# A two-layer decoder on one core: one shared block result kept in SBUF and added by VectorE, the turning block emptied by ScalarE, one chunk's bank taken from the other PSUM pool

## The chip, the core and the metric

The kernel runs on one core of a Trainium2 chip. The metric is the device time of one execution in microseconds. A core has TensorE (PE in the profile, with its weight loads as PEld), VectorE (DVE), ScalarE (ACT), GpSimd (POOL) and SyncE (SP). They run their own instruction streams and wait for each other on semaphores; data moves between DRAM and SBUF by DMA, and the matmuls write into PSUM, which here is eight banks of 128 x 512 fp32.

## The reference

Two layers of a hybrid decoder over 512 tokens of width 1024, all in fp32, and a final RMSNorm:

```
h   = RMSNorm(x)
z   = h @ W_in      # attn q,k,v | ret q,k,v,g | gate_a | gate_b
A   = sliding-window attention with rotary q/k and sinks
B   = retention with group norm and swish gate
y   = sigmoid(gate_a) * (A @ W_a) + sigmoid(gate_b) * (B @ W_b)
x   = x + y @ W_out
x   = x + relu(RMSNorm(x) @ W_up)^2 @ W_down     # 1024 -> 4096 -> 1024
```

The change touches the second half, the MLP (`W_up`, `W_down`), the first products of a layer (`W_in`, the attention's q) and the final RMSNorm.

## The kernel before

**Products.** fp32 operands are split into a high and a low part (`split_until`: ScalarE makes `hi` at L308, VectorE `lo` at L309; for activations L361/L362 and L364/L365), and each product is three matmuls, high x high, high x low and low x high (`products`, L354 to L356). Raw weights come by SP's queue into a ring of five tiles, `hi` and `lo` have rings of four; sums of weight blocks that are needed come from DRAM and are added with L267 and L290. The scheduler of the framework decides the order in which each engine takes its instructions, from the program's order and its own estimates.

**Banks.** Five of the eight PSUM banks belong to the pool `ps_mm`, three to `ps_aux`. `temp()` gives a 128 x 512 tile from a ring of seven in SBUF: who takes the eighth waits until the first one's readers are done, DMAs out of it among them.

**The start of a layer.** `group` takes four `ps_mm` banks for the products of k, v and two chunks of q (`put_k`, `put_v`, `put_q(0)`, `put_q(1)`), then `chunk` takes one bank each for q(2) and q(3). `rotate` reads a bank (L566, L567 by ScalarE, L570 by VectorE) and applies the rotary tables; `beside` spreads the results by SP's DMAs (L597). The scores are L705.

**The MLP.** It is cut into eight blocks e of hidden units. Each block has two `pair` products (up, with relu and square) and one `down` product. Both are multiplications of 2 x 2 blocks in seven products instead of eight, so the results share partial sums:

- `pair` holds three half banks a, e, b in `ps_mm`. It copies a to b on ScalarE (L1152), copies e to the tile `eu` (L1154), copies b there (L1157), and goes on accumulating in all three; L1159, L1164, L1166, L1167 and L1172 finish the squares.
- `down` holds four `ps_mm` banks a[0..1], c[0..1] and two `ps_aux` banks b[0..1]; b begins as a copy of a (L1234). It yields results (i, j, m), where i is the half of the tokens' columns, j and m choose one of four output blocks. Two of them are early: `early(1, 1)` from c and `early(0, 1)` from b are partial sums shared with later results; then come `put(0, 0)` from a, `put(0, 1)` from c, `put(1, 1)` from b and `put(1, 0)` from b, with another product into b before each of the last two.

**Adding** (blocks 0 to 6 of each layer): each of the twelve results of a block (six names, two values of m) is taken out of PSUM by ScalarE into a tile (L1276) and sent by POOL with an accumulating DMA into a DRAM tensor y (L1278). (1, 1) and (0, 1) are thus each sent twice, once for the early part and once for the late one. POOL waits before an accumulating DMA until the earlier one into the same place has landed.

**Ending** (block 7 of each layer): y comes back from DRAM (L1292) and VectorE adds the last results from PSUM (`add`, L1307). In layer 0 the early (1, 1) is still added by an accumulating DMA (L1303), `turn` transposes the results on TensorE (L1334) and adds them to x (L1340), and `carry`, which runs inside layer 1's first group, turns the half i = 1; behind it x is split into xh (L364) and xl (L365) for the next products. In layer 1 the Ending also makes the final RMSNorm: squares on ScalarE (L1315), the gain on VectorE (L1316), the root and its inverse, the scaling on VectorE for i = 1 (L1323) and on ScalarE for i = 0 (L1326), and the DMAs to the output.

Of the kernel before, what the change touches and what calls it, by code (L numbers as in the profile page):

```python
# [12 lines left out]
AF = mybir.ActivationFunctionType  # L13
ALU = mybir.AluOpType
# [4 lines left out]
T = 512  # L19
# [95 lines left out]
def decoder(ctx, tc, xT, x_first, w_in, w_a, w_b, w_out, w_up, w_pair, w_down, w_end, tables, decay, band, g_last, out):  # L115
    nc = tc.nc
# [19 lines left out]
    def bank(pool, name):  # L136
        return pool.tile([P, T], F32, tag=pool.name, name=name)
# [229 lines left out]
    xs = [(xh[:, k, :], xl[:, k, :]) for k in range(KD)]  # L367
# [4 lines left out]
    def advance(rate=1.0):  # L372

        credit[0] += rate
        while credit[0] >= 1.0:
            credit[0] -= 1.0
            while background:
                try:
                    next(background[0])
                    break  # L380
                except StopIteration:
                    background.pop(0)
# [2 lines left out]
        while background:  # L385
            advance()

    def chunk(name, layer, moving, evacuate, rate=1.0):

        hi, lo = unit(name, layer)  # L390
        n = len(moving)
        ps = bank(ps_mm, "mm")
        pairs = [((hi[:, k * P : (k + 1) * P], lo[:, k * P : (k + 1) * P]), moving[k]) for k in range(n)]
        advance(rate)
        products(ps, pairs[: n // 2], True, False)
        advance(rate)
        products(ps, pairs[n // 2 :], False, True)
        evacuate(ps)
# [150 lines left out]
    def layer_body(layer):  # L549
# [81 lines left out]
        def put_q(c):  # L631
            def put(ps):
                r = rotate(ps, attn_tabs, layer == 0 and c < 2)
                if c % 2 == 0:
                    qlo[:] = [big("qlo")]
                lo = qlo[0][:, c % 2, :]
                for g in range(N_KV):
                    nc.scalar.activation(q_s[g][:, c, :], r, AF.Copy)
                nc.vector.tensor_tensor(lo, r, f32(q_s[0][:, c, :]), ALU.subtract)
                for g in range(N_KV):  # L640
                    beside(g, q_s[g][:, c, :], lo)

            return put
# [6 lines left out]
            {0: squares, 1: rms_mix.prepare, 2: stats} if layer == 0 else {0: carried.pop(), 2: rms_mix.prepare, 3: stats},  # L650
        )
        chunk("w_in", layer, xs, put_q(2))
        chunk("w_in", layer, xs, put_q(3))
        turn_v()

        a_t = [slots.four() for _ in range(2)]
# [187 lines left out]
        class Head:  # L844


            def __init__(self, h):
                self.h = h
# [193 lines left out]
        last = layer == DEPTH - 1  # L1042
        y = dram.tile([P, NB, D], F32, name=f"y{layer}")
# [7 lines left out]
        factor, negative = (columns[:, i * NB : (i + 1) * NB] for i in range(2))  # L1051
        if last:
# [3 lines left out]
            last_gain = gain_tile[:, 0:2, :]  # L1056
# [199 lines left out]
        class Adding:  # L1256


            def __init__(self, e):
                self.e = e  # L1260

            def last_but_one(self):
                pass
# [2 lines left out]
                pass  # L1266

            def early(self, i, j, m, ps, sign):
                self.send(i, j, m, temp("eu"), ps, sign, last or self.e > 0)

            def put(self, i, j, m, ps, sign):
                self.send(i, j, m, temp("y"), ps, sign, last or self.e > 0 or j == 1)

            def send(self, i, j, m, t, ps, sign, add):
                block = 2 * j + m
                nc.scalar.activation(t, ps, AF.Copy, scale=(factor if sign > 0 else negative)[:, block : block + 1])  # L1276
                how = {"accum_op": ALU.add} if add else {}
                nc.gpsimd.dma_start(y[:, block, i * T : (i + 1) * T], t, **how)  # L1278

        class Ending:  # L1280


            def __init__(self):
                self.y, self.done = {}, set()
# [23 lines left out]

            def put(self, i, j, m, ps, sign):
                block = 2 * j + m  # L1310
                self.add(i, j, m, ps, (factor if sign > 0 else negative)[:, block : block + 1])
                if last:
                    v = self.y[i, j, m]
                    first, total, both = (sq[:, n * NB + block : n * NB + block + 1] for n in range(3))
                    nc.scalar.activation(temp("junk"), v, AF.Square, accum_out=both if i else first)  # L1315
                    nc.vector.tensor_tensor(v, v, last_gain[:, i, :], ALU.mult)  # L1316
# [6 lines left out]
                    nc.vector.tensor_scalar(v, v, total, None, ALU.mult)  # L1323
# [28 lines left out]
                    carried.append(self.carry)  # L1352

            def carry(self):
                for half in range(2):
                    for j in (1, 0):
                        self.turn(1, j, half, ps_aux)
                    for k in (4 + 2 * half, 5 + 2 * half):
                        scaled_input(k, g_mix + 2)
                for k in range(KD):  # L1360
                    squared_input(k, g_mix + 2)
                    nc.sync.dma_start(spill[:, k, :], x[:, k, :])
                late_box[0] = late_tile(F32R)
                slots.add(late_box[0])
# [200 lines left out]
```

## Time and profile before

| | |
|---|---|
| Runs | 1497.24, 1502.52, 1502.98 us; median 1502.52 |
| Profiled execution | 1501.42 us |
| Its span | 1499.7 us |
| Mean granted TensorE clock | 0.997 |
| DMA moved | 286.25 MB, mean 191 GB/s |

The span runs from the first to the last instruction; the profiled execution's own time has 1.72 us around it. In rows of a timeline the first number is the start in us from the span's start, the second the duration, and a bracket at the end names the idle time of the engine ahead of the instruction and what ended it. In a group's row stand its count, its busy time in us, the mean of one in ns, and the engine's idle time ahead of it. Matmul rows overlap: their pitch, not their duration, is what a product costs.

### The profile page before, as it was taken

To read this page: it belongs to the slowest core of one execution; us is meant where nothing else is said; L and a number is where in the kernel's file an instruction comes from. 1 tells how busy PE (TensorE), PEld (TensorE's weight loads), DVE (VectorE), ACT (ScalarE), POOL (GpSimd) and SP (SyncE) were. 2 spreads that over 40 slices of the span, in tenths; PEclk is the share of its full clock that TensorE was granted. 3 is DMA by queue.
4 is the path that set the end of the run, shared out by engine and by line. 5 is a ranking of instruction groups with operands and counts; after the bars stand their busy time and mean duration, and the time that the engine had idled before them with its cause. 6 is when DMAs were issued, how large, how long until landed. Compare 5 with 4: busy or idle time off the path is not lost.

```text
span 1499.7 us, 21303 instructions
## 1 busy us (share of the span) xinstructions
PE 1471.8 (98%) x7787; PEld 1265.7 (84%) x7787; DVE 1044.3 (70%) x1589; ACT 940.9 (63%) x1551; POOL 239.7 (16%) x334
## 2 busy tenths in 40 slices
PE   9999999999999999999999999999999999999997
PEld 7888888888889999998778888888888789888885
DVE  6878568654677777776977775677447677777665
ACT  7657355532568888887755563555325778877775
POOL 0101121101002222223001011111000212222230
PEclk9999999999999999999999999999999999999999
DMA  7654997668227888888836579876443488888883
GB/s 257 189 169 113 303 256 185 185 179 223 92 72 220 211 215 218 223 213 230 290 100 182 147 207 273 223 205 155 140 121 110 122 205 213 210 219 211 218 205 126
DMA packets 100472, 286.25 MB, mean 191 GB/s; under 512 B 11664, under 2 KB 11792, under 8 KB 96528
## 3 DMA queue, kind: packets, MB, share of 16 engines
q0 software_dynamic: 38832, 114.31, 36.3%
q1 hardware_dynamic: 60816, 169.27, 33.5%
q8 instruction: 61, 1.00, 0.3%
q10 hardware_dynamic: 720, 1.31, 0.2%
q14 instruction: 43, 0.35, 0.1%
HBM read 231.37 MB, written 113.77 MB: 230 GB/s over the span
## 4 chain that ended last, share of the span: by engine, by line
PE 87%; DMA 6%; ACT 3%; DVE 2%; issue 2%; DVEq 0%; ACTq 0%
PE mm L354 23%; PE mm L355 23%; PE mm L356 23%; DMA raw<-w_down_in 3%; DMA raw<-w_pair_in 2%; PE rv L354 2%; PE rv L356 2%; PE rv L355 2%; PE b L354 2%; PE b L355 2%; PE b L356 2%; DVE lo L309 1%; PE score L705 1%; ACT hi L308 1%; PE pT L670 1%
## 5 line engine op out<-in xcount | busy, mean ns | idle before, releaser
L308 ACT ACTIVATE hi<-raw 128x1024 fp32r<-128x1024 f32 (+1 forms) x363 | 369.8, 1020 | 324.4 <-PE mm L355 195.4
L309 DVE TENSOR_TENSOR lo<-raw,hi 128x1024 fp32r<-128x1024 f32 (+1 forms) x364 | 424.5, 1170 | 201.9 <-ACT hi L308 199.8
L354 PE MATMUL mm<-xh,hi 128*128 128x512 f32 (+1 forms) x1008 | 358.4, 359 | 14.4 <-ACT eu L1154 9.5
L355 PE MATMUL mm<-xl,hi 128*128 128x512 f32 (+1 forms) x1008 | 356.9, 356 | 0.0
L356 PE MATMUL mm<-xh,lo 128*128 128x512 f32 (+1 forms) x1008 | 356.2, 356 | 0.7 <-DVE lo L309 0.7
L354 PE MATMUL mm<-r,hi 128*128 128x256 f32 (+1 forms) x736 | 238.7, 324 | 0.5 <-ACT mm L1152 0.5
L356 PE MATMUL mm<-r,lo 128*128 128x256 f32 (+1 forms) x736 | 238.9, 325 | 0.0
L355 PE MATMUL mm<-r,hi 128*128 128x256 f32 (+1 forms) x736 | 238.8, 324 | 0.0
L354 PEld LDWEIGHTS mm<-xh,hi 128*128 128x128 f32 x1008 | 190.7, 189 | 44.2 <-ACT eu L1154 12.5
L356 PEld LDWEIGHTS mm<-xh,lo 128*128 128x128 f32 x1008 | 190.7, 189 | 26.2 <-DVE lo L309 0.9
L355 PEld LDWEIGHTS mm<-xl,hi 128*128 128x128 f32 x1008 | 191.0, 189 | 25.5 <-DVE xl L365 0.2
L354 PEld LDWEIGHTS mm<-r,hi 128*128 128x128 f32 x736 | 139.8, 190 | 13.7 <-ACT mm L1152 0.7
L355 PEld LDWEIGHTS mm<-r,hi 128*128 128x128 f32 x736 | 139.8, 190 | 13.1
L356 PEld LDWEIGHTS mm<-r,lo 128*128 128x128 f32 x736 | 139.8, 190 | 11.3
L1278 POOL DMA_DIRECT2D y<-eu x56 | 47.3, 851 | 387.7 <-ACT eu L1276 383.4
L1278 POOL DMA_DIRECT2D y<-y x112 | 98.1, 1257 | 66.4 <-DMA y<-eu 35.5
L355 PE MATMUL mm<-lo,r 128*128 128x512 f32 x272 | 104.2, 392 | 0.0
L356 PE MATMUL mm<-hi,r 128*128 128x512 f32 x272 | 100.7, 390 | 0.0
L354 PE MATMUL mm<-hi,r 128*128 128x512 f32 x272 | 97.8, 393 | 0.2
L267 DVE TENSOR_TENSOR raw<-raw 128x512 f32<-128x512 f32 x56 | 38.5, 688 | 67.6 <-DMA raw<-sums_up 54.1
L354 PE MATMUL b<-hi,r 128*128 128x512 f32 x180 | 70.5, 392 | 1.6 <-DVE y L1307 1.6
L355 PE MATMUL b<-lo,r 128*128 128x512 f32 x180 | 70.3, 390 | 0.0
(262 smaller groups left out, 2314.3 us busy)
## 6 DMA issues: line engine op xcount, KB each, us to landing
raw<-w_in_in SPq DMA_DIRECT2D x89, 512.0 KB, 5.5
sums_down<-w_down_in POOLq DMA_DIRECT2D x30, 1024.0 KB, 11.3
y<-y POOLq DMA_DIRECT2D x120, 256.0 KB, 7.9
sums_up<-w_pair_in POOLq DMA_DIRECT2D x56, 512.0 KB, 9.8
raw<-w_down_in SPq DMA_DIRECT2D x45, 512.0 KB, 8.7
raw<-w_pair_in SPq DMA_DIRECT2D x84, 256.0 KB, 4.2
raw<-sums_down SPq DMA_DIRECT2D x30, 512.0 KB, 9.1
y<-eu POOLq DMA_DIRECT2D x58, 256.0 KB, 5.8
```

The costliest lines, as they stand in the source:

```text
L267: nc.vector.tensor_tensor(raws[i][:, at], last[:, LEFT], last[:, RIGHT], ALU.add)
L308: nc.scalar.activation(hi[:, at], raw[:, at], AF.Copy)
L309: nc.vector.tensor_tensor(lo[:, at], raw[:, at], f32(hi[:, at]), ALU.subtract)
L354: nc.tensor.matmul(ps, ah, bh, start=start and i == 0, stop=False, **more)
L355: nc.tensor.matmul(ps, ah, bl, start=False, stop=False, **more)
L356: nc.tensor.matmul(ps, al, bh, start=False, stop=stop and i == n - 1, **more)
L670: nc.tensor.transpose(pt[:, i * P : (i + 1) * P], sm[:, at : at + P], ident)
L705: nc.tensor.matmul(ps[:, g * w : (g + 1) * w], q_s[g][:, c, at], part[:, keys], start=i == 0, stop=i == 1)
L1278: nc.gpsimd.dma_start(y[:, block, i * T : (i + 1) * T], t, **how)
```

## The change

Four edits:

1. In Adding, the tiles of `early(1, 1)` are kept (`kept`) and not sent. At `put(1, 1)` VectorE adds the scaled bank into the kept tile with one scalar_tensor_tensor, and the tile is sent once. A block has ten accumulating DMAs instead of twelve, and ten ScalarE evacuations instead of twelve. In the first block of layer 0, where the first DMA into a place writes instead of adding, (1, 1) now writes.
2. In the Ending of layer 0, `put(1, 1)` is taken out of PSUM by ScalarE into tiles `aside`, and `carry` adds these on VectorE (two tensor_tensor from SBUF) ahead of the turns; the turns there go in the order j = 0, 1 instead of 1, 0.
3. In the Ending of layer 1, for i = 1 the gain multiplication is joined with the scaling, in one scalar_tensor_tensor: four VectorE multiplications fewer.
4. `chunk` gets a pool, and q(3) of each layer takes its bank from `ps_aux`.

```
-    def chunk(name, layer, moving, evacuate, rate=1.0):
+    def chunk(name, layer, moving, evacuate, rate=1.0, pool=ps_mm):
...
-        ps = bank(ps_mm, "mm")
+        ps = bank(pool, "mm")
...
-        chunk("w_in", layer, xs, put_q(3))
+        chunk("w_in", layer, xs, put_q(3), pool=ps_aux)
...
             def early(self, i, j, m, ps, sign):
-                self.send(i, j, m, temp("eu"), ps, sign, last or self.e > 0)
+                t = self.evacuated(j, m, temp("eu"), ps, sign)
+                if i:
+                    self.kept[m] = t
+                else:
+                    self.send(i, j, m, t, last or self.e > 0)
 
             def put(self, i, j, m, ps, sign):
-                self.send(i, j, m, temp("y"), ps, sign, last or self.e > 0 or j == 1)
-
-            def send(self, i, j, m, t, ps, sign, add):
+                t = self.kept[m]
+                if (i, j) == (1, 1):
+                    nc.vector.scalar_tensor_tensor(t, ps, self.scale(j, m, sign), t, ALU.mult, ALU.add)
+                else:
+                    t = self.evacuated(j, m, temp("y"), ps, sign)
+                self.send(i, j, m, t, last or self.e > 0 or (i, j) == (0, 1))
+
+            def scale(self, j, m, sign):
                 block = 2 * j + m
-                nc.scalar.activation(t, ps, AF.Copy, scale=(factor if sign > 0 else negative)[:, block : block + 1])
+                return (factor if sign > 0 else negative)[:, block : block + 1]
+
+            def evacuated(self, j, m, t, ps, sign):
+                nc.scalar.activation(t, ps, AF.Copy, scale=self.scale(j, m, sign))
+                return t
+
+            def send(self, i, j, m, t, add):
                 how = {"accum_op": ALU.add} if add else {}
-                nc.gpsimd.dma_start(y[:, block, i * T : (i + 1) * T], t, **how)
+                nc.gpsimd.dma_start(y[:, 2 * j + m, i * T : (i + 1) * T], t, **how)
...
             def put(self, i, j, m, ps, sign):
                 block = 2 * j + m
-                self.add(i, j, m, ps, (factor if sign > 0 else negative)[:, block : block + 1])
+                scale = (factor if sign > 0 else negative)[:, block : block + 1]
+                if not last and (i, j) == (1, 1):
+                    t = self.aside[m] = temp("eu")
+                    nc.scalar.activation(t, ps, AF.Copy, scale=scale)
+                else:
+                    self.add(i, j, m, ps, scale)
                 if last:
...
-                    nc.vector.tensor_tensor(v, v, last_gain[:, i, :], ALU.mult)
                     if not i:
+                        nc.vector.tensor_tensor(v, v, last_gain[:, i, :], ALU.mult)
...
-                    nc.vector.tensor_scalar(v, v, total, None, ALU.mult)
+                    nc.vector.scalar_tensor_tensor(v, v, total, last_gain[:, 1, :], ALU.mult, ALU.mult)
...
             def carry(self):
+                for m in range(2):
+                    v = self.y[1, 1, m]
+                    nc.vector.tensor_tensor(v, v, self.aside[m], ALU.add)
                 for half in range(2):
-                    for j in (1, 0):
+                    for j in range(2):
                         self.turn(1, j, half, ps_aux)
```

The instructions of the engines also come in another order than before, since the scheduler works the order out anew. In each steady block TensorE does the third product into b ahead of the second one into e; on ScalarE the copy L1154 of a block's first pair stands behind two more weight splits; on POOL the DMAs of (1, 1) stand ahead of the second one of (0, 1).

More of the change, by code (lines that the diff above doesn't have):

```diff
@@ L1259, in __init__ @@
             def __init__(self, e):
-                self.e = e
+                self.e, self.kept = e, {}
             def last_but_one(self):
@@ L1268, in early @@
             def early(self, i, j, m, ps, sign):
-                self.send(i, j, m, temp("eu"), ps, sign, last or self.e > 0)
-            def put(self, i, j, m, ps, sign):
-                self.send(i, j, m, temp("y"), ps, sign, last or self.e > 0 or j == 1)
-            def send(self, i, j, m, t, ps, sign, add):
-                block = 2 * j + m
-                nc.scalar.activation(t, ps, AF.Copy, scale=(factor if sign > 0 else negative)[:, block : block + 1])
+                t = self.evacuated(j, m, temp("eu"), ps, sign)
[3 more added lines that the diff above has]
+                    self.send(i, j, m, t, last or self.e > 0)
+            def put(self, i, j, m, ps, sign):
+                t = self.kept[m]
[5 more added lines that the diff above has]
+            def scale(self, j, m, sign):
+                block = 2 * j + m
+                return (factor if sign > 0 else negative)[:, block : block + 1]
[3 more added lines that the diff above has]
+            def send(self, i, j, m, t, add):
                 how = {"accum_op": ALU.add} if add else {}
-                nc.gpsimd.dma_start(y[:, block, i * T : (i + 1) * T], t, **how)
+                nc.gpsimd.dma_start(y[:, 2 * j + m, i * T : (i + 1) * T], t, **how)
         class Ending:
             def __init__(self):
-                self.y, self.done = {}, set()
+                self.y, self.aside = {}, {}
                 for i, j in ((1, 1), (0, 1), (0, 0), (1, 0)):
```

## The prediction

> **What bounds the kernel now.** I read the page first, then TensorE's waits, then windows over blocks.
>
> ```profile
> span 1499.7 us, 21303 instructions
> PE 1471.8 (98%) x7787; PEld 1265.7 (84%) x7787; DVE 1044.3 (70%) x1589; ACT 940.9 (63%) x1551; POOL 239.7 (16%) x334
> ...
> PE 87%; DMA 6%; ACT 3%; DVE 2%; issue 2%; DVEq 0%; ACTq 0%
> ```
>
> The number of matmuls does not change, so the only thing to win or lose is TensorE's idle time: 1499.7 − 1471.8 = 27.9 us, the start and the tail included. That is the ceiling of any gain. The engines that the change relieves, ScalarE (63%) and POOL (16%), are not the bound as engines; they count only where TensorE waits for them. Where it waits:
>
> ```profile
> PE mm L354 <- ACT eu L1154: 9.5, 9, 2.0
> PE mm L354 <- DVE rot L570: 2.8, 1, 2.8
> PE mm L354 <- ACT xh L364: 2.0, 2, 1.3
> PE b L354 <- DVE y L1307: 1.6, 1, 1.6
> ```
>
> (total us, times, longest.) Nine waits for one copy of the pair stage, and three single ones. The windows say in which blocks:
>
> ```profile
> 579.00:618.50 39.50, 39.50 (x256) 36.09 (x255) 29.48 (x38) 32.47 (x54) 11.39 (x16) 1.00 0.88 217
> ...
> 1301.00:1321.00 20.00, 20.00 (x106) 17.12 (x106) 19.08 (x25) 17.96 (x31) 3.92 (x5) 1.00 0.61 164
> 1321.00:1342.00 21.00, 20.41 (x155) 19.51 (x154) 11.20 (x14) 15.10 (x26) 6.61 (x8) 1.00 1.07 251
> ```
>
> (Window: length, busy PE, PEld, DVE, ACT, POOL, granted clock, DMA share, GB/s.) A steady block of layer 0 has TensorE busy without a hole; a block of layer 1 loses 0.59 us, in its second half. The DMA engines are loaded unevenly: 0.61 in the half with the down product, 1.07, that is full, in the other.
>
> **The change, part by part.**
>
> *q(3) in the other pool.* The four products of the group and q(2) hold the five ps_mm banks, so q(3) waited until VectorE (L570) had read the first one:
>
> ```profile
> 770.46 0.39 PE L356 MATMUL mm<-xh,lo 128*128 128x512 f32 x1
> 773.67 0.80 PE L354 MATMUL mm<-xh,hi 128*128 128x512 f32 x1 [2.83 <-DVE rot L570]
> 774.27 0.63 PE L355 MATMUL mm<-xl,hi 128*128 128x512 f32 x1
> ...
> 776.68 0.39 PE L355 MATMUL mm<-xl,hi 128*128 128x512 f32 x1
> ...
> 789.40 0.33 PE L705 MATMUL score<-r,r 128*128 128x128 f32 x2
> ```
>
> From 770.46 to 776.68 there are eight steps in 6.22 us; at the pitch of the rows after it (0.23) they take 1.82. So 4.4 us are lost: the gap, and about 1.4 us behind it, in which a matmul takes 0.63 instead of 0.39. A ps_aux bank is free there, so all of it can go. Some is given back: the first score moves from 789.40 to 785.0 and needs the rotated q and k, and VectorE, busy with the rotations, is not made faster.
>
> ```profile
> 772.94 0.68 DVE L570 TENSOR_TENSOR rot<-mm,tab 128x512 f32<-128x512 f32 x1
> ...
> 781.52 2.44 SPq L597 DMA_DIRECT2D r<-qlo x4
> ...
> r<-qlo SPq DMA_DIRECT2D x4, 64.0 KB, 2.0
> ```
>
> The last of these four is issued by 781.52 + 2.44 = 783.96 and lands up to 2.0 later, at 785.4 to 786.0: 0.4 to 1.0 after the new need. I take −3.4; bounds −4.4 (nothing given back) and 0 (the scores wait for VectorE all the same).
>
> The Trainium skill (TensorE: Matmul & The Clock Gate, "HAM oscillation — how this bites in real kernels") asks for no idle gap over about 3.4 us, which would leave the 2.83 us gap without a clock penalty; its Part 1 calls the window free-running. By that rule the term would be about −3.0 before what is given back, by the trace it is −4.4; the trace decides.
>
> *Ten accumulating DMAs.* The two dropped per Adding block are those of early(1,1):
>
> ```profile
> 1311.87 0.86 POOL L1278 DMA_DIRECT2D y<-eu  x1 [1.17 <-ACT eu L1276]
> 1317.92 0.86 POOL L1278 DMA_DIRECT2D y<-eu  x1 [5.19 <-ACT eu L1276]
> ```
>
> The second of them is issued at 1311.87, six us ahead of the next y DMA, in the half where the DMA share is 0.61. The full half keeps its ten. I cost the 28 DMAs at 0; their cover is that light half, and if they did delay the loads it would be a gain (rival A).
>
> *(1,1) added by VectorE.* The exchange, from the groups by form:
>
> ```profile
> L308 ACT ACTIVATE hi<-raw 128x1024 fp32r<-128x1024 f32 x330 | 349.3, 1059 | 304.4 <-PE mm L355 192.5 <-issue 45.4 <-PE mm L356 26.0
> ...
> L1276 ACT ACTIVATE y<-b,columns 128x512 f32<-128x512 f32 x56 | 38.9, 695 | 27.4 <-DMA y<-y 12.4 <-DMA y<-eu 11.3 <-PE b L356 2.5
> ...
> L308 ACT ACTIVATE hi<-raw 128x512 fp32r<-128x512 f32 x33 | 20.6, 625 | 20.0 <-DMA raw<-w_pair_in 15.4 <-PE mm L355 2.9 <-PE mm L356 0.9
> ...
> L1307 DVE SCALAR_TENSOR_TENSOR late<-mm,columns,late 128x512 f32<-128x512 f32 x4 | 2.9, 740 | 0.0
> ```
>
> ScalarE loses 28 evacuations of 0.695 us, VectorE gains 28 of 0.740 (the same form with the sum in SBUF). In the second half of the block VectorE is busy 11.20 of 21.00 us, so two more (1.5 us) have room, and they also free the b banks without a tile of the ring: cost 0. If b came free late, each late tenth would stand in front of the third product into b; bounds 0 to +1.5 per block, taken 0.
>
> The Trainium skill (VectorE: DVE Perf Modes, "Specifications") places ScalarE closer to PSUM and VectorE closer to SBUF, which speaks against moving this read. The rows differ by 0.045 us, 1.3 us of VectorE over 28; as a charge on the path it would add that much to the sum, as the trace has it the engine is idle there.
>
> *The order that follows.* The schedule moves things: TensorE does the third product into b ahead of e; on ScalarE, y01's second evacuation now waits for the landing of eu(0,1) (before, y11's did, at the same place in time); and L1154 of pair 0, which stood right behind the last evacuation, now stands behind two weight splits, hi of 512 and of 1024 columns. The last evacuation still waits for y00's landing (its tile of the ring), so L1154 ends at the start of that evacuation plus 0.59 + 0.53 + 0.95 + 0.39 = 2.46 us (the durations of the rows above less the 0.1 by which neighbours overlap, and L1154's own 0.39, in the rows below). TensorE needs it 14 matmuls of 0.12 us, 1.68 us, after the start of the xh group.
>
> ```profile
> 538.14 0.69 ACT L1276 ACTIVATE y<-b,columns 128x512 f32<-128x512 f32 x1 [1.20 <-DMA y<-y]
> ...
> 578.38 0.69 ACT L1276 ACTIVATE y<-b,columns 128x512 f32<-128x512 f32 x1 [0.77 <-DMA y<-y]
> 579.66 0.39 ACT L1154 ACTIVATE eu<-mm 128x256 f32<-128x256 f32 x1 [0.60 <-DMA y<-y]
> ```
>
> ```profile
> 538.77 0.28 PE L354 MATMUL mm<-xh,hi 128*128 128x256 f32 x1
> ...
> 578.66 0.28 PE L354 MATMUL mm<-xh,hi 128*128 128x256 f32 x1
> ```
>
> One block: 538.14 + 2.46 = 540.60 against 538.77 + 1.68 = 540.45, a new stall of 0.15. The next: 580.84 against 580.34, 0.50. Six such blocks in layer 0 have no slack to spend: 0.9 to 3.0, taken +2.0. In layer 1 each block already waits, later, for a load of weights that TensorE's lateness does not move (the 0.59 us above), which swallows a stall of this size: 0, bounds 0 to +3.5 (0.5 in seven blocks).
>
> *Layer 0's end and layer 1's end.*
>
> ```profile
> 712.62 0.39 PE L354 MATMUL mm<-xh,hi 128*128 128x256 f32 x1 [1.80 <-ACT eu L1154]
> ```
>
> ```profile
> 1462.63 1.06 ACT L308 ACTIVATE hi<-raw 128x1024 fp32r<-128x1024 f32 x1 [1.68 <-DMA raw<-w_end_in]
> ```
>
> In front of the 1.80 us wait now stand 12 more matmuls of 0.12 us, 1.44 us of cover: −1.4, bounds −1.8 and +1. The end of layer 1 waits for a load that the change does not touch: −0.3, bounds −2.0 and +1.
>
> *The turning block, at the layer boundary.*
>
> ```profile
> 734.99 0.47 PE L354 MATMUL b<-hi,r 128*128 128x512 f32 x1 [1.57 <-DVE y L1307]
> ...
> 740.53 1.19 PE L354 MATMUL mm<-xh,hi 128*128 128x512 f32 x4 [1.32 <-ACT xh L364]
> ...
> 742.85 0.50 PE L355 MATMUL mm<-xl,hi 128*128 128x512 f32 x1
> ```
>
> ```profile
> 734.10 0.74 DVE L1307 SCALAR_TENSOR_TENSOR y<-b,columns,y 128x512 f32<-128x512 f32 x1
> ...
> 738.47 1.27 DVE L1340 TENSOR_TENSOR x<-x,turn 128x512 f32<-128x512 f32 x2
> ...
> 742.05 1.40 DVE L365 SCALAR_TENSOR_TENSOR xl<-x,xh 128x512 fp32r<-128x512 f32 x2
> ```
>
> ScalarE empties b early, so the 1.57 us wait goes. But none of these VectorE rows has an idle time: it works straight through to the first xl at 742.05, which TensorE takes at 742.85. Ahead of that xl two sums of 0.66 (pitch) become two adds of 0.60, and, with the carry's order turned, seven turn adds stand there instead of five: −0.12 + 1.20 = +1.1. What TensorE wins at b it loses waiting for xl. Taken +1.1; bounds −2.9 (both waits go and VectorE isn't late) and +2.3 (one more pair of adds).
>
> *The tail.* VectorE has the last word:
>
> ```profile
> 1492.04 0.65 DVE x L1307
> 1492.69 0.60 DVE x L1316
> ...
> 1493.42 0.39 DVE x L1323
> ```
>
> Four gain products (0.60) go, four scalings (0.39) become three-operand forms (0.65): −2.4 + 1.0 = −1.4; I take −1.3, bounds −1.4 and −0.5 (the last sum waits for TensorE instead).
>
> Sum: −3.4 + 0 + 0 + 2.0 + 0 − 1.4 − 0.3 + 1.1 − 1.3 = −3.3. The profiled execution took 1501.42 us (1.7 more than its span); 1501.4 − 3.3 = 1498.1. The median shown, 1502.52, is 1.1 above it, and the fastest run 4.2 below it, so I stay with 1498.
>
> **The rivals.**
>
> A: the dropped DMAs empty the queue after all. Each moves 256 KB to memory and reads what is there; with less ahead of them, eu(0,1) and y00 land earlier, and the weights of layer 1 with them. Then the new stalls of layer 0 (2.0) don't come, and of the 9.5 us at L1154 the 1.8 of layer 0's end are already counted and the rest goes: 1498.1 − 2.0 − 7.7 = 1488.4. For it: the share of 1.07 in the half where the waits are. Against: the two come and go in the other half.
>
> B, the slower side: y00 lands later. POOL now issues y11's DMAs ahead of y01's second, some 2 us sooner, into the full half. If that costs y00 one place in the queue (1.28 us, from 578.38 to 579.66, two evacuations released by successive landings), L1154 behind the two splits is late by 0.33 + 1.28 = 1.6 us in six blocks and 0.5 + 1.28 = 1.8 in seven, 22.1; layer 1's 7.7 us of later waits swallow their part: 14.4. It decides from a landing under 0.78 us (2.46 − 1.68) ahead of the xh group, and the rows have 0.63 and 0.28: there is no reserve. 1498.1 − 2.0 + 14.4 = 1510.5. Against: the queue seems to land in the order of issue.
>
> C: the change does not do what it says. VectorE, not the bank, sets the start of attention, so the 3.4 come back as a wait of the scores: 1498.1 + 3.4 = 1501.5.
>
> **How the numbers follow.** My forecast 0.52, own range 1490 to 1504 (its terms' bounds, not all at one end); A 0.19, B 0.21, C 0.08. The range reaches down to A and up to B: 1488 to 1511. About 0.5%, 7.5 us, is what a measurement of this kernel can tell from no change: faster means below 1495.0, slower above 1510.0. Faster: A and two fifths of the forecast, whose gains are surer than its losses, 0.40; slower: three quarters of B, since its price has no upper end at one place, 0.16; within: the rest, 0.44.
>
> **What would show it.** Right: no wait of q(3) on L570 and no rows of 0.63 us around 774; new waits of 0.1 to 0.5 us on L1154 at the xh group of layer 0's blocks, where there are none now; no wait of b on L1307 near 735, and a later xl; a tail with four gain products fewer. Wrong: L1154's waits gone in layer 1 (A), over 1 us in each block (B), scores that wait near 786 (C), or waits of b on the new VectorE sums inside a block.

## The result and the profile after

The changed kernel takes 1494.90 us (median of six runs, 1492.88 to 1496.50), the kernel before 1500.03 us on the same chip (six runs, 1497.24 to 1502.98): a ratio of 0.9965, with a 95% interval of 0.9948 to 0.9981. A second set of runs gave 1494.31 us and 0.9963 (0.9948 to 0.9978). That is 5 us faster, a small difference but clear of the noise, and below the 0.5% of the prediction.

The profiled execution took 1495.45 us. From its page:

```profile
span 1493.7 us, 21278 instructions
...
PE 1474.4 (99%) x7787; PEld 1268.8 (85%) x7787; DVE 1065.9 (71%) x1613; ACT 924.2 (62%) x1525; POOL 217.2 (15%) x306
```

VectorE has 21.6 us more, ScalarE 16.7 and POOL 22.5 less, as the edit says. TensorE's idle time (span less busy) went from 27.9 to 19.3 us, but its busy time rose by 2.6 us at the same count of matmuls: some of them ran at a slower pace, 0.63 us each in place of 0.39 (below). TensorE's waits (total us, times, longest):

```profile
PE mm L354 <- ACT hi L308: 5.0, 11, 0.7
PE turn L1354 <- DVE y L1322: 1.6, 1, 1.6
...
PE mm L354 <- ACT xh L364: 0.9, 2, 0.6
PE mm L355 <- DVE xl L365: 0.7, 1, 0.7
PE mm L354 <- ACT eu L1154: 0.5, 1, 0.5
```

The 9.5 us at L1154 are down to 0.5, the wait of q(3) on L570 is gone, and a new group of eleven short waits for a weight split (hi, L308) has come. The windows of one block of layer 0 and of the two halves of one of layer 1:

```profile
594.00:634.00 40.00, 39.65 (x256) 36.09 (x255) 31.87 (x40) 31.84 (x53) 8.79 (x10) 1.00 0.76 204
1300.63:1320.63 20.00, 20.00 (x105) 17.14 (x104) 18.42 (x25) 17.08 (x28) 3.48 (x4) 1.00 0.38 119
1320.63:1340.58 19.95, 19.54 (x152) 18.85 (x152) 12.81 (x16) 13.97 (x24) 5.32 (x6) 1.00 1.09 271
```

The two dropped DMAs left the half that was light already (a DMA share of 0.61 before, 0.38 now); the full half is as full as it was (1.07, 1.09). Layer 0 now loses 0.35 us in a block where it lost nothing, layer 1 loses 0.41 in its second half where it lost 0.59. The two halves are one block of layer 1; over all its blocks layer 1 wins far more, as the next table shows.

To compare kernels, I cut each trace at the start of the first matmul of every block's down product (the first mm<-hi,r of L354 in it). "Layer 0" runs from the first block's to the seventh's, "end" from there to the eighth's, "between" from there to layer 1's first block and holds the layer boundary and q(3), "layer 1" from its first block's to its eighth's. Behind that all have the same 24.9 us to TensorE's last matmul, and then the tail.

| kernel | start | layer 0 | end | between | layer 1 | tail |
|---|---|---|---|---|---|---|
| before | 435.9 | 234.7 | 43.6 | 463.1 | 288.2 | 9.2 |
| changed | 437.9 | 236.1 | 42.9 | 461.7 | 282.3 | 8.0 |
| changed_again | 437.9 | 236.1 | 42.9 | 461.6 | 282.5 | 8.0 |
| traffic_back | 437.6 | 236.6 | 42.9 | 459.8 | 283.2 | 8.0 |
| adding_alone | 435.6 | 236.2 | 42.7 | 461.9 | 282.5 | 9.2 |
| without_adding | 436.0 | 235.7 | 44.4 | 460.1 | 288.5 | 8.0 |
| order_alone | 437.8 | 234.4 | 44.1 | 464.8 | 279.2 | 9.2 |
| kept_big | 436.2 | 233.4 | 42.4 | 459.8 | 277.6 | 8.9 |
| kept_big_again | 435.9 | 233.1 | 42.2 | 461.7 | 278.7 | 8.9 |
| kept_big_turn | 438.0 | 233.6 | 42.4 | 458.8 | 277.4 | 8.9 |
| kept_big_j | 437.6 | 233.6 | 42.3 | 459.8 | 277.5 | 9.0 |
| order_pool_tail | 435.9 | 233.8 | 43.8 | 458.8 | 280.0 | 8.0 |

In the changed kernel the gain lies in layer 1, −5.9 us, where the prediction had next to none. Against it stand +2.0 before the first block and +1.3 in layer 0. The 2.0 are lost in the first 10 us, ahead of anything that the change touches.

**q(3).** The last matmul of q(2) and the first of q(3), in the timeline of the changed kernel:

```profile
776.13 0.39 PE L356 MATMUL mm<-xh,lo 128*128 128x512 f32 x1
776.36 0.39 PE L354 MATMUL mm<-xh,hi 128*128 128x512 f32 x1
```

No gap, no rows of 0.63. Matched matmul by matmul, 4.4 us are won here, and behind the attention the difference is the same: nothing is given back.

**The xh group in a block of layer 0**, ScalarE and then TensorE:

```profile
580.36 0.69 ACT L1288 ACTIVATE y<-b,columns 128x512 f32<-128x512 f32 x1 [0.77 <-DMA y<-y]
580.95 1.57 ACT L308 ACTIVATE hi<-raw 128x512 fp32r<-128x512 f32 x2
582.41 0.37 ACT L1154 ACTIVATE eu<-mm 128x256 f32<-128x256 f32 x1
```

```profile
580.61 0.28 PE L354 MATMUL mm<-xh,hi 128*128 128x256 f32 x1
...
582.57 0.39 PE L354 MATMUL mm<-xh,hi 128*128 128x256 f32 x1 [0.36 <-ACT hi L308]
```

The last evacuation waits for y00's landing, two splits stand between it and L1154, and TensorE waits 0.36 us, twelve matmuls after the group's start (the prediction counted fourteen). This is the wait the prediction described, only that TensorE waits there for the second of the two splits itself and not for L1154 behind it.

**The load in layer 1.** VectorE of before and then of the changed kernel, at the same place of the same block:

```profile
1325.17 0.69 DVE L267 TENSOR_TENSOR raw<-raw 128x512 f32<-128x512 f32 x1 [4.31 <-DMA raw<-sums_up]
1325.78 1.22 DVE L309 TENSOR_TENSOR lo<-raw,hi 128x1024 fp32r<-128x1024 f32 x1
1327.66 0.69 DVE L267 TENSOR_TENSOR raw<-raw 128x512 f32<-128x512 f32 x1 [0.66 <-DMA raw<-w_pair_in]
```

```profile
1323.32 0.69 DVE L267 TENSOR_TENSOR raw<-raw 128x512 f32<-128x512 f32 x1 [2.50 <-DMA raw<-sums_up]
1323.92 2.35 DVE L309 TENSOR_TENSOR lo<-raw,hi 128x1024 fp32r<-128x1024 f32 x2
1326.20 0.68 DVE L267 TENSOR_TENSOR raw<-raw 128x512 f32<-128x512 f32 x1
```

Before, one split, then a sum that waits for a load, then the next split. Now the two splits come first. The second one is the last reader of a raw tile, and SP's next load waits for that tile: after, the splits end at 1323.92 + 2.35 = 1326.27, and the load is issued at 1326.31. SP, before and after:

```profile
1329.52 0.33 SPq L261 DMA_DIRECT2D raw<-w_pair_in  x1
1330.12 0.33 SPq L284 DMA_DIRECT2D raw<-w_down_in  x1
```

```profile
1326.31 0.33 SPq L261 DMA_DIRECT2D raw<-w_pair_in  x1
1328.68 0.33 SPq L284 DMA_DIRECT2D raw<-w_down_in  x1
```

Counted from the block's cut (1302.32 in the one trace, 1300.63 in the other), the load at L261 is issued after 27.2 and after 25.7 us, 1.5 earlier (2.1 in the block before this one). The first load of w_down is issued at about the same 27.8 and 28.1, but it lands earlier: 36.2 us after the cut in this block as in the one before it, against 37.3 and 37.7. With the other load gone ahead sooner, less of that is still in front of it; this is the likely reason, and no run singles it out. ScalarE's split of that load, before and after:

```profile
1339.69 1.06 ACT L308 ACTIVATE hi<-raw 128x1024 fp32r<-128x1024 f32 x1 [1.32 <-DMA raw<-w_down_in]
```

```profile
1336.94 1.06 ACT L308 ACTIVATE hi<-raw 128x1024 fp32r<-128x1024 f32 x1
```

Before, ScalarE sat 1.32 us waiting for the load, and L1154 stood right behind this split. TensorE waited for it:

```profile
1341.07 0.39 PE L354 MATMUL mm<-xh,hi 128*128 128x256 f32 x1 [0.58 <-ACT eu L1154]
```

After, there is no such wait. What made the load early was still open here: the order, or the two DMAs that are gone.

**The boundary**, TensorE and VectorE of the changed kernel:

```profile
741.79 0.98 PE L1354 MATMUL turn<-ident,y 128*128 128x128 f32 x7 [1.63 <-DVE y L1322]
...
746.57 0.80 PE L355 MATMUL mm<-xl,hi 128*128 128x512 f32 x1 [0.74 <-DVE xl L365]
747.17 0.63 PE L356 MATMUL mm<-xh,lo 128*128 128x512 f32 x1
```

```profile
743.97 1.89 DVE L1360 TENSOR_TENSOR x<-x,turn 128x512 f32<-128x512 f32 x3
745.76 1.42 DVE L365 SCALAR_TENSOR_TENSOR xl<-x,xh 128x512 fp32r<-128x512 f32 x2
```

The wait at b is gone; a turn waits in its place, and the first xl comes behind seven turn adds where it came behind five. Then matmuls run at 0.63 us for 2.6 us. Matched against before, the boundary is 3.0 us longer.

**The tail.** The last pieces of the chain:

```profile
1486.47 0.67 DVE x L1322
...
1488.91 0.75 DVE x L1343
```

One sum, the square on ScalarE, and one joined product behind it, in place of the row of gain products: the span ends 8.0 us after TensorE's last matmul in place of 9.2.

### The profile page after: what moved, and what is told of

It reads as the page before. It is cut to its first block, busy times and chain, and to the rows that moved or that the text cites. A ratio compares the mean times of both kernels' runs of the same rounds, so it can differ in the third digit from the quotient of the medians.

```text
span 1493.7 us, 21278 instructions
## 1 busy us (share of the span) xinstructions
PE 1474.4 (99%) x7787; PEld 1268.8 (85%) x7787; DVE 1065.9 (71%) x1613; ACT 924.2 (62%) x1525; POOL 217.2 (15%) x306
## 4 chain that ended last, share of the span: by engine, by line
PE 69%; issue 17%; DMA 8%; ACT 4%; DVE 2%; POOL 1%; POOLq 0%; ACTq 0%; DVEq 0%
PE mm L354 19%; PE mm L355 18%; PE mm L356 18%; DMA y<-y 6%; PE rv L354 2%; PE rv L356 2%; PE rv L355 2%; DMA y<-eu 2%; ACT hi L308 2%; PE score L705 1%; PE pT L670 1%; POOL y L1293 1%; PE r L355 1%; PE r L356 1%; PE r L354 1%
## 5 line engine op out<-in xcount | busy, mean ns | idle before, releaser
L308 ACT ACTIVATE hi<-raw 128x1024 fp32r<-128x1024 f32 (+1 forms) x363 | 368.4, 1019 | 314.0 <-PE mm L355 208.0
L354 PE MATMUL mm<-xh,hi 128*128 128x512 f32 (+1 forms) x1008 | 358.3, 359 | 6.6 <-ACT hi L308 5.0
L354 PE MATMUL mm<-r,hi 128*128 128x256 f32 (+1 forms) x736 | 238.5, 324 | 0.5 <-ACT mm L1152 0.5
L354 PEld LDWEIGHTS mm<-xh,hi 128*128 128x128 f32 x1008 | 191.2, 190 | 35.5 <-ACT hi L308 7.5
L356 PEld LDWEIGHTS mm<-xh,lo 128*128 128x128 f32 x1008 | 190.7, 190 | 26.1 <-DVE lo L309 0.6
L354 PEld LDWEIGHTS mm<-r,hi 128*128 128x128 f32 x736 | 139.7, 190 | 13.6 <-ACT mm L1152 0.7
L1293 POOL DMA_DIRECT2D y<-eu x56 | 52.7, 1089 | 423.8 <-ACT eu L1288 416.9
L354 PE MATMUL mm<-hi,r 128*128 128x512 f32 x272 | 97.8, 393 | 0.2
L1293 POOL DMA_DIRECT2D y<-y x84 | 77.1, 1054 | 48.3 <-DMA y<-eu 18.2
L354 PE MATMUL b<-hi,r 128*128 128x512 f32 x180 | 70.5, 392 | 0.0
L356 PE MATMUL b<-hi,r 128*128 128x512 f32 x180 | 67.8, 389 | 0.0
```

The lines of the kernel that those rows point to most:

```text
L308: nc.scalar.activation(hi[:, at], raw[:, at], AF.Copy)
L354: nc.tensor.matmul(ps, ah, bh, start=start and i == 0, stop=False, **more)
L356: nc.tensor.matmul(ps, al, bh, start=False, stop=stop and i == n - 1, **more)
L1293: nc.gpsimd.dma_start(y[:, 2 * j + m, i * T : (i + 1) * T], t, **how)
```

## The experiments

**Is it the DMA traffic? (traffic_back)** The changed kernel, with the kept tiles also sent, accumulating, into a spare tensor; line numbers are one higher in it.

```
                 if i:
                     self.kept[m] = t
+                    nc.gpsimd.dma_start(spare[:, m, :], t, accum_op=ALU.add)
```

> The changed kernel, with the two dropped DMAs of a block put back: the kept tiles of early (1,1) are also sent, accumulating, into a spare DRAM tensor that nothing reads. Each engine's order inside a block stays that of the changed kernel. Theory O (order): layer 1's blocks are shorter than before because VectorE takes a weight split ahead of a sum that waits for a load (L309 ahead of L267), so a raw tile comes free 2 us earlier and the loads behind it land earlier; the two DMAs move in a light stretch and cost nothing. Then layer 1's steady blocks stay at 40.0 us (+-0.15), the first load of w_down lands 36.2 us (+-0.5) after the block's start, and the time is within 1 us of the changed kernel's 1494.9. Rival A (traffic): the freed DMA time is what moved the loads. Then blocks of layer 1 go back towards 40.4, w_down lands near 37.6, and the time is 3 to 6 us longer.

Measured: 1494.72 us (ratio 0.9957, 0.9942 to 0.9971). In the block before the one shown above, the load of w_down lands 36.2 us after the cut, as in the changed kernel and as the order would have it. Layer 1 is 283.2 us, and 2.3 of these are a wait that no other trace has, for VectorE's new sum (L1280 here), in layer 1's first block:

```profile
PE mm L355 <- ACT hi L309: 3.6, 9, 0.5
PE b L355 <- DVE eu L1280: 2.5, 2, 2.3
```

The later blocks took 39.3 to 40.1 us, less than the changed kernel's 39.9 to 40.2 and in part below the 40.0 expected, not the 40.4 of rival A. The 28 DMAs can come back and the steady blocks of layer 1 keep their gain: the traffic is not what moved the load, and rival A falls. The wait of b for VectorE's sum shows that this edit can hold b, as the prediction feared; it happened in one block, only here, and why is open.

**The first edit alone (adding_alone)** The class Adding of the change in the kernel before; the rest untouched.

```
                 if i:
+                    self.kept[m] = t
...
+                if (i, j) == (1, 1):
+                    nc.vector.scalar_tensor_tensor(t, ps, self.scale(j, m, sign), t, ALU.mult, ALU.add)
```

> The kernel before with the first edit alone (kept tile, VectorE's sum, ten DMAs). Theory O and A both put the whole shift of the blocks here: layer 0's six steady blocks 1.3 us longer together (waits of 0.36 at the xh group), layer 1 from its first block to its last about 6 us shorter, the q(3) wait of 2.8 and the tail as before; together about 1495.5. If instead the blocks' gain needs the other edits (another place of the scheduler's order), layer 1 stays at the length of before and the time at 1500.

Measured: 1497.79 us (0.9980, 0.9966 to 0.9994); the profiled execution took 1494.66. The stages are as expected: layer 0 +1.5, layer 1 −5.7, the end −0.9; "between" is 1.3 shorter, for a reason told below, and the tail is as before.

```profile
PE mm L354 <- ACT hi L308: 4.8, 11, 0.8
PE mm L354 <- DVE rot L570: 2.8, 1, 2.8
```

So the whole shift in the blocks belongs to the kept tile. The expected total of 1495.5 was lower than the median: −5.1 in the stages against −2.7 in the medians. The profiled execution was one of the two fastest of ten. Single traces and medians differ by a few us here, and I lean on the stages; by the medians alone, the other three edits (without_adding, −4.8) would have won more than this one.

This trace shows one more thing. It has the same gap of 2.83 us before q(3), but behind it the matmuls go at the full pace:

```profile
773.92 0.50 PE L354 MATMUL mm<-xh,hi 128*128 128x512 f32 x1 [2.83 <-DVE rot L570]
774.26 0.39 PE L355 MATMUL mm<-xl,hi 128*128 128x512 f32 x1
```

Of the 4.4 us that the gap cost in the trace of before, 1.3 were a slower pace that does not always come. (order_alone, below, has the same gap too, and the slow pace behind it.)

**All but the first edit (without_adding)** The changed kernel with the class Adding of before.

```
             def early(self, i, j, m, ps, sign):
+                self.send(i, j, m, temp("eu"), ps, sign, last or self.e > 0)
```

> The changed kernel with the twelve DMAs and twelve evacuations of before in Adding: edits 2 to 4 alone. q(3) -3.5, tail -1.3, and the layer boundary, which the changed kernel's trace shows 2 us longer at the first xl, +1.4 with layer 0's end: 1500.0 - 3.4 = about 1496.6. The blocks of both layers have the lengths of before (39.4 and 40.3). If the boundary is not the turning block's doing but the Adding part's, this one comes out near 1494.5.

Measured: 1495.72 us (0.9973, 0.9959 to 0.9986); the profiled execution took 1499.30, one of the slowest. The blocks of layer 1 have their old length (288.5 in all) and TensorE its old waits:

```profile
PE mm L354 <- ACT eu L1154: 8.8, 10, 2.0
```

q(3) is 4.4 us shorter, the tail 1.3, and the boundary 1.4 longer, 0.5 of it slow pace that reaches over from the end of layer 0; without that, 0.9. Layer 0 came out at 235.7, with two waits of 0.5 at L1154 where before has one of 0.3: even an unchanged Adding has such blocks, so a single trace's layer 0 is uncertain by about 1 us.

**Is it the order? (order_alone)** The kernel before, with VectorE's second L267 of a pair put behind the split that frees the raw tile. No other engine's order changes.

```
+            with tc.issue_after(lows[i - 4].ins) if order[i][3] == 2 and order[i - 4][1] == "pair" else nullcontext():
-            nc.vector.tensor_tensor(raws[i][:, at], last[:, LEFT], last[:, RIGHT], ALU.add)
+                nc.vector.tensor_tensor(raws[i][:, at], last[:, LEFT], last[:, RIGHT], ALU.add)
...
-                nc.vector.tensor_tensor(lo[:, at], raw[:, at], f32(hi[:, at]), ALU.subtract)
+                lows[i] = nc.vector.tensor_tensor(lo[:, at], raw[:, at], f32(hi[:, at]), ALU.subtract)
```

> The kernel before with one thing changed: in each pair of blocks VectorE takes the weight split (L309) that frees a raw tile ahead of the sum (L267) that waits for a load, as the changed kernel's schedule does; every other engine's order, the twelve DMAs and all the arithmetic are those of before. Theory O: the load at L261 is issued about 2 us earlier in a block (25.4 us after the block's start, not 27.45), the first load of w_down lands about 36.2 and not 37.3 to 37.7 after it, and layer 1, from its first block's down product to its last's (288.2 us before), loses 4 to 6 us, since L1154 stands where it stood and adds no wait; layer 0 stays at 39.4 a block. About 1495.5. Rival (the evacuations): the loads move because ScalarE's and POOL's order changed; then layer 1 stays within 1 us of 288.2 and the time at 1500.

Measured: 1492.43 us (0.9956, 0.9940 to 0.9973), 3 us below what was expected. The instructions of TensorE, ScalarE, POOL and SP come in the same order as before. VectorE and SP in the same block:

```profile
1325.59 2.35 DVE L309 TENSOR_TENSOR lo<-raw,hi 128x1024 fp32r<-128x1024 f32 x2
1327.86 0.68 DVE L267 TENSOR_TENSOR raw<-raw 128x512 f32<-128x512 f32 x1
```

```profile
1327.97 0.33 SPq L261 DMA_DIRECT2D raw<-w_pair_in  x1
1329.17 0.33 SPq L284 DMA_DIRECT2D raw<-w_down_in  x1
```

```profile
PE mm L354 <- ACT eu L1154: 3.0, 5, 1.8
```

Both loads are early, the waits at L1154 shrink from 9.5 to 3.0 us (1.8 of them are the end of layer 0, which this does not touch), and a block of layer 1 takes 39.4 to 39.75 us:

```profile
1302.23:1341.61 39.38, 39.38 (x254) 35.95 (x253) 29.75 (x38) 32.24 (x54) 10.55 (x12) 1.00 0.87 217
```

The load at L261 went 25.4 us after the cut, as expected, and w_down landed at 35.6, a little earlier than the 36.2 expected. Layer 1 lost 9.0 us, more than the 4 to 6 expected. Here no split stands in front of L1154, so the waits at the xh group do not come. Its trace has slow pace at the start, behind the wait at the end of layer 0 and behind q(3)'s gap, so its span (1494.4 us) shows less of the gain than the median. One swap of two VectorE instructions in a block, with every DMA left in, thus gives as much as the whole change (1492.43 against 1494.31 on the same chip; the intervals overlap); the rival (ScalarE's and POOL's order) falls, since these are those of before.

**Is it the ring? (kept_big)** The changed kernel with the two kept tiles in one tile of the ring of six large ones.

```
                 if i:
-                    self.kept[m] = t
+                    if not m:
+                        self.both = big("kept")
+                    self.kept[m] = self.evacuated(j, m, self.both[:, m, :], ps, sign)
```

> The changed kernel with the kept tiles of early (1,1) in one tile of the ring of six large tiles, and no longer in the ring of seven: y10's second evacuation then waits for the landing of eu(0,1), some 4 us earlier, and not of y00, and L1154 not for y00's second one. If the ring is what holds the two splits and so TensorE at the xh group (waits of 0.36 to 0.68 in 12 blocks, 5.0 us on hi L308), these waits go: 4 to 5 us less than the changed kernel, about 1490.5. If in layer 1 the next wait, for the load of w_down, takes their place, only layer 0's 1.9 us and a little of layer 1 are won: about 1493.

Measured: 1486.19 us (0.9912, 0.9887 to 0.9937); again, 1486.07 (0.9900, 0.9887 to 0.9914). More than expected. All eleven waits at the xh group went, in both layers, and no other took their place. A block of layer 0 and one of layer 1:

```profile
590.85:630.18 39.33, 39.33 (x255) 35.82 (x253) 31.72 (x40) 32.29 (x53) 8.80 (x10) 1.00 0.77 204
1292.38:1331.63 39.25, 39.25 (x254) 35.90 (x253) 30.72 (x40) 31.29 (x52) 8.80 (x10) 1.00 0.77 204
```

TensorE is busy without a hole in each. The last evacuation ahead of the two splits, which in the changed kernel waited for y00's DMA, now waits only for its bank:

```profile
575.09 0.69 ACT L1290 ACTIVATE y<-b,columns 128x512 f32<-128x512 f32 x1 [0.67 <-PE b L356]
```

So the eleven waits of 0.35 to 0.68 were the ring of seven: y10's second evacuation waited for a tile whose DMA was late, with the splits queued behind it. (The scheduler's order moved a little here as well, but the two splits still stand between that evacuation and L1154.) 2.7 us came from layer 0, 4.7 from layer 1. This is faster than both kernels, although the tail is 0.9 longer than the changed kernel's in all four traces with the large ring; that lies behind the last product, and its cause is open.

> The kernel with the kept tiles in the large ring again, on the same chip as order_pool_tail, for the comparison: about 1486.2, layer 1 at 277.6 us and layer 0 at 233.4, and the first xl at the boundary about 1.1 us later than before.

The second run had layer 0 at 233.1 and layer 1 at 278.7 us; its boundary was 3.0 us longer than before's, not 1.1, with the slow pace in it.

**The turning block (kept_big_turn, kept_big_j)** The kernel with the large ring, in one with edit 2 undone, in the other with the edit but the carry in the order j = 1, 0.

```
-                    for j in range(2):
+                    for j in (1, 0):
                         self.turn(1, j, half, ps_aux)
```

> The kernel with the kept tiles in the large ring, and the turning block of layer 0 as before (VectorE adds from PSUM, the carry in the order 1, 0): edit 2 undone. If edit 2 costs what the traces of the runs with it and without it show (first xl matmul 1.0 later), this one is 1.0 us faster than the one with it: about 1485.2, its trace with waits of 1.57 and 1.3 at the boundary and the later of layer 1's products 1.0 us earlier. If the boundary's cost was the other edits' doing, it stays at 1486.2.

> The kernel with the kept tiles in the large ring, with the turning block emptied by ScalarE as in the change, but the carry's turns in the order 1, 0 of before. If the two more turn adds ahead of the first xl are the cost of the boundary, as the prediction has it, the stretch from the last product into b to the first group's fourth weight unit is about 1 us shorter than with the order 0, 1. If the adds of the tiles set aside are the cost, it stays the same.

Measured: 1486.44 us (0.9914, 0.9901 to 0.9927) and 1486.37 (one run). Neither time differs from kept_big's. In the traces, the stretch with the boundary is 1.0 us shorter with edit 2 undone (458.8 against 459.8) and has the waits of 1.57 and 1.32 back, as expected, and it is unchanged with the order turned back (459.8). In that kernel, too, VectorE has seven turn adds ahead of the first xl, because the scheduler put them there: the order of j as written is not the cause, and the run can't tell the adds of the tiles set aside from the two more turn adds. The gain of 1 us by the trace is not resolved by the times.

**The slow pace (changed_again)** The changed kernel as it is, once more.

> The changed kernel a second time. Its first trace has matmuls of 0.63 us in place of 0.39 from 747.2 to 749.7 and some 2 us of them in the first 10 us. If these are a draw of the execution and not the change's, one or both are gone here, and the span is 2 to 4 us shorter than 1493.7, with the blocks' lengths (39.9, 40.1) and the waits on hi L308 as they were.

Measured: 1494.31 us, with a span of 1493.9 in the profiled execution. Every stage is within 0.2 us of the first trace, and the slow pace is there again, at both places:

```profile
746.65 0.79 PE L355 MATMUL mm<-xl,hi 128*128 128x512 f32 x1 [0.74 <-DVE xl L365]
747.24 0.63 PE L356 MATMUL mm<-xh,lo 128*128 128x512 f32 x1
```

The expectation that one or both would be gone failed. Behind the first xl the slow pace came in three of the seven traces that have edit 2 (both of the changed kernel, and kept_big_again), and not in traffic_back, without_adding, kept_big and kept_big_j. The granted clock, third from the end in a window's row, tells more: it falls to 0.50 at the boundary in five of the seven, for 3.41 us in kept_big and kept_big_j and for 6.83 in the other three. kept_big and its repeat are the same kernel, and in the first the clock is back before the products with xl:

```profile
738.25:741.66 3.41, 2.93 (x8) 2.00 (x8) 3.41 (x6) 3.41 (x7) 0.00 (x0) 0.50 0.97 336
```

```profile
742.03 0.40 PE L356 MATMUL mm<-xh,lo 128*128 128x512 f32 x1
```

```profile
738.22:745.05 6.83, 6.07 (x17) 4.08 (x16) 6.83 (x12) 6.83 (x13) 0.00 (x0) 0.50 0.92 328
```

```profile
742.02 0.63 PE L355 MATMUL mm<-xl,hi 128*128 128x512 f32 x1
```

The boundary of kept_big is 1.1 us longer than before's, as is that of traffic_back, whose clock does not fall there: the shorter stretch eats into TensorE's wait for xl (0.51 us in kept_big, 1.20 in traffic_back) and costs nothing more. For that kernel the longer stretch is a draw, of 1.9 us: it comes in one execution and not in another; that both traces of the changed kernel have it does not show that all its executions do. At the start it is a draw too: about 2 us are lost in the first 10 us in six of the twelve traces and not in the other six, kernels with and without the change among both, and all twelve begin with the same instructions. (There the granted clock in the windows reads 1.00 in both sorts, and only the matmul rows show the pace.)

**Is the kept tile needed? (order_pool_tail)** The kernel before with the swap of order_alone, q(3) in the other pool and the joined gain.

```
+        chunk("w_in", layer, xs, put_q(3), pool=ps_aux)
...
+                    nc.vector.scalar_tensor_tensor(v, v, total, last_gain[:, 1, :], ALU.mult, ALU.mult)
```

> The kernel before with VectorE's order swapped as in order_alone, q(3) in the other pool and the joined gain of the last layer: neither the kept tile nor the turning block's edit. If the swap is what the kept-tile edit was worth, and q(3) and the tail add up as their stages show (-4.4, of which up to 1.3 is a draw, and -1.3), this is 1492.4 - 5 = about 1487, with layer 1 near 279 us and layer 0 near 234.5: as fast as the kept tiles in the large ring without any of the twelve DMAs dropped. If dropping the DMAs is worth something beside the order, it stays 2 us or more behind the run with the large ring.

Measured: 1488.76 us (0.9912, 0.9898 to 0.9927), on a chip and against runs of before where kept_big_again had 1486.07 (0.9900, 0.9887 to 0.9914). 12 us faster than before without the kept tile, but 2.7 behind the large ring by the medians; the intervals overlap. The two traces don't show that difference in their spans (1485.1 us here, 1485.4 there). By stages, this kernel is behind by 0.7 in layer 0, 1.5 at its end and 1.3 in layer 1, and ahead by 2.9 between (1.9 of it the draw that kept_big_again has) and 0.9 in the tail. In the blocks, then, the kept tile in the large ring is worth some 3.5 us beside the order, less than the order itself; as a whole the two kernels are not clearly told apart.

## Why the prediction came out right, point by point

The forecast was 1498, by −3.3 us on the profiled execution; the measured difference of the medians was −5.1, of the traces −6.0. It holds, but partly by luck: one large term was missed, and a slower pace of TensorE at two places, which no term stood for, offset a part of it.

- **q(3), −3.4.** −4.4: the bank was the whole cause, and the 1.0 that I took off for the scores' operands was not needed. 1.3 of it is the slower pace, which adding_alone, with the same gap, did not have and order_alone had; the part that is sure is 3.1.
- **28 DMAs at 0.** Right within what the runs resolve: with the traffic put back, the time is the same, layer 0 is 0.5 us longer and the steady blocks of layer 1 are no longer.
- **(1, 1) on VectorE at 0.** Right in the changed kernel, whose trace has no wait of b on it; traffic_back had one of 2.3 us.
- **The new wait at the xh group, layer 0, +2.0.** +1.3 in the stage (adding_alone +1.5), and one more wait of 0.36 falls into the end of layer 0. Mechanism and place right; what TensorE waits for is the second split, not L1154, which ends 0.27 us later.
- **Layer 1 at 0.** This step failed: −5.9. The prediction said that each block of layer 1 waits "for a load of weights that TensorE's lateness does not move". TensorE's lateness does not, but VectorE's order does, and I had not followed the raw tile from the split that frees it to the load that takes it. The orders of TensorE, ScalarE and POOL were compared ahead of the run, and VectorE's was not among them. In a sum that asks what each edit costs, a side effect of the scheduler on an engine that no edit was meant to speed up had no line.
- **The end of layer 0, −1.4.** The wait of 1.80 us is 0.48, −1.3. The stage as a whole is 0.7 shorter, with the new wait of 0.36 in it.
- **The end of layer 1, −0.3.** The wait of 2.02 us behind the load of w_end is gone, within the −5.9; the same failed step.
- **The boundary, +1.1.** +1.1 in kept_big, kept_big_j and traffic_back, +0.9 in without_adding; +3.0 in the changed kernel, the rest being the slow pace. The sum of turn adds and xl was right to a tenth; whether the two more turn adds or the adds of the tiles set aside make it, no run tells.
- **The tail, −1.3.** −1.3, as reckoned.
- **Rival A** had the right effect (L1154's waits gone in layer 1) with the wrong cause. **Rival B** did not come: in layer 1, in the block before the one shown, y00 lands 26.2 us after the cut, and landed after 26.1; in the block shown of layer 0 it is 26.0 in both. The two splits alone cost the 0.36. **Rival C** did not come: nothing was given back at the scores.

With −5.9 in place of the two terms for layer 1 (0 and −0.3), the forecast would have been −3.3 − 5.6 = −8.9. The draws of pace, +2.0 and +1.9 in this trace and 1.3 at q(3) in the trace of before, take 2.6 off that, and made the sum look better than its steps. That the measured −5.1 lies so near −3.3 is in part luck.

## What to carry to other kernels

Where a tile framework works out the order, a change's largest effect can be a swap on an engine that the edit does not aim at: compare the orders and follow each freed buffer to the load that waits for it, before pricing the edits. A tile kept longer in a ring is paid for by whoever takes the tile after it; with the kept tile in a ring with room, the whole change was worth 14 us in place of 5. And compare traces stage by stage, since two draws of 2 us in a single execution are as large as most of the effects here, and look at the granted clock of the stage before giving a longer stage to an edit.

## What the runs showed of the hardware

Behind waits of TensorE under 3 us the granted clock fell to 0.50, for 3.41 us or for twice that, and a matmul of 128x512 then took 0.63 us (0.39 otherwise). Behind q(3)'s gap of 2.83 us in the trace of before:

```profile
773.09:776.50 3.41, 2.83 (x7) 2.25 (x8) 3.41 (x6) 2.28 (x4) 0.00 (x0) 0.50 0.50 159
```

order_alone has it behind the same gap, adding_alone does not; without_adding has it behind single gaps of 1.80 and 2.03, traffic_back behind one of 2.33. At the boundary it came behind gaps of 1.63 and 0.36 (or thereabouts) with short transposes between them, in five of the seven traces with edit 2. The Trainium skill (TensorE: Matmul & The Clock Gate, Part 1) calls the activity window free-running, 3413 ns long; the stretches of 3.41 and 6.83 us agree with it, and it fits a draw that depends on where the gap falls. The rule of that page to have no idle gap over about 3.4 us ("HAM oscillation — how this bites in real kernels") is too lax here: gaps of 1.80 to 2.83 us were enough.
